# A hybrid attention layer in one kernel: one product of ones per gated norm, transposes taken in pairs, and head 0's mixes, its v and the end's logarithm in other places

## The chip, the cores and the metric

The kernel runs on one core of a Trainium2 chip. The metric is the time of one execution on the device in microseconds (us). The engines are named as in the profile: PE is TensorE (matrix products and transposes), PEld its weight loads, DVE is VectorE, ACT is ScalarE, POOL is GpSimd, SP is SyncE, which here only issues DMA transfers. Each engine works off its own queue of instructions in order and waits for others through semaphores.

## The reference

One layer of a decoder trunk: 1024 positions, width 1024, eight heads of differential softmax attention beside four heads of gated linear attention (GLA), all in float32. Cut to what matters:

```python
h = rms_norm(x, pre_g)
z = h @ w_in                        # qa ka va ga | qb kb vb gb gk_low
# differential attention, 8 heads, two maps of 64 each, v of 128
p = softmax(where(mask, s, -inf))   # for both maps, causal
w = p[:, :, 0] - lam * p[:, :, 1]
oa = rms_norm(w @ v, subln_g) * (1 - lam_init) * silu(ga)
# gated linear attention, 4 heads, keys of 128, values of 256
ob = gla_chunked(qb, kb, vb, log_sigmoid(gk) / 16)
ob = rms_norm(ob, gla_g) * silu(gb)
y = concatenate([oa, ob]) @ w_out
return x + rms_norm(y, post_g)
```

## The kernel before

Float32 accuracy is reached by splitting: an operand is cast to a rounded form (`_hi`) and the rest (`_lo`) is what the cast left; products of hi and lo parts are summed in a PSUM bank. So each operand costs a cast on ACT and a subtraction on DVE.

The work has four stages by the trace: the loads and the first norm (to 16 us), the projections with GLA between them (to 616 us), the attention (616 to about 912 us), and the last products and the final norm (to 963 us). Everything is written as generators that yield costs; a merger interleaves them, and a scheduler then sets the order on each engine, except for instructions marked `keep_in_program_order`, which stay in order among themselves. `issue_after(x)` puts an instruction behind x.

In GLA, each of eight units (four heads, two halves of the positions) ends in a norm: the squares of its 256 values lie as two tiles of 128 rows, which are added to `sq`, split into `sq_hl` (hi and lo, 128 rows each), and summed over the rows by two products with a matrix of ones, into a bank called `gms`. In the attention the same norm (`attn_norm`, bank `ms`) already folds its 128 rows to 64, and puts hi and lo one below the other, so that one product does.

The attention's streams:

- `scores(h, qb)`: for head h and query block qb (7 down to 0), the scores of both maps m into one of three banks `sc`, then on DVE a masked reduce to `p0` or `p1` (the custom instruction, printed ISA in the order of instructions), which also leaves a bound in `stt`; on ACT the Exp, which leaves the sum of a row in `stt`; on DVE the RECIPROCAL of both maps' sums; on POOL p1 times lambda; on DVE the mix of both maps (SCALAR_TENSOR_TENSOR `p<-p,stt,p`). In head 0 the mixes of the blocks above 3 are held in a list and made behind a later block's reduce.
- `all_values()`: for each head, half 1 of the queries and then half 0, in units of one block of keys (the last unit has two): `turn` transposes the mixed maps into one of two banks `wtr` (TR) and takes them out as `wt_hi` (cast on ACT) and `wt_lo` (DVE); `weigh` multiplies with v into the one bank `po`. Transposes run two units ahead. At the end of a half `po` is copied to `o`, which frees the bank, and the norm follows; its result, `gate`, is stored to `mixd`. The norm's bank `ms` is taken in turn from the same two as the transposes.
- early products of the output projection (`ypart`, `yps`), which fill TensorE's time between the scores. From about 793 us on they also use the attention's own results, which are loaded from `mixd` as `m_raw` and split into `m_hi` and `m_lo` in `mix_part`.

Loads by SP wait for each other only through their data and through the buffers that they fill. `turned_last` and `squared_last` name the instructions behind which some of the end's ACT work is held.

Of the kernel before, what the change touches and what calls it, by code (L numbers as in the profile page):

```python
# [14 lines left out]
P = 128  # L15
# [16 lines left out]
def hymba_kernel(  # L32
# [44 lines left out]
    def fp(t):  # L77
        return t.bitcast(F32)
# [930 lines left out]
    def gla(g):  # L1009

        u = None
        for half in range(2):
# [72 lines left out]
            dve.tensor_tensor(sq, sqs[:, 0], sqs[:, 1], ALU.add)  # L1085
            hl = kp.tile([P, 2, 512], F32R, tag="k1", name="sq_hl")
            act.copy(hl[:, 0], sq)
            dve.tensor_tensor(hl[:, 1], sq, fp(hl[:, 0]), ALU.subtract)
            for _ in range(2 if last else 3):
                yield  # L1090
            ms, ib = take_bank([P, 512], "gms")
            for i in range(2):
                mm(ms, ones, hl[:, i], start=(i == 0), stop=(i == 1))
            r = t_c("r")
# [143 lines left out]
    def load_v(h):  # L1238
        v = [smp.tile([P, NT, P], F32R, tag="v", name=f"v{t}", bufs=4) for t in range(2)]
        for t in range(2):  # L1240

            with tc.issue_after(qk_load[0]) if h else nullcontext():
                ins = sp.dma_start(fp(v[t]), v_d[h // 4][h % 4, t])
            if h == 0:
                tc.keep_in_program_order(ins)
        return v

    v_first = load_v(0)

# [13 lines left out]
    def scores(h, qb):  # L1263
# [6 lines left out]
        for m, p in enumerate((p0, p1)):  # L1270
# [5 lines left out]
            for i, (a, b) in enumerate(parts):  # L1276
# [21 lines left out]
                if (h, qb) == (0, NT - 1):  # L1298
                    lowest[:] = [ins.ins]
                c = 0.08 + (e - a) / 512 * 0.56  # L1300
                if last:
                    act.activation(
                        p[:, :n], p[:, :n], AF.Exp, bias=st[:, m : m + 1], scale=-1.0,
                        accum_out=st[:, 2 + m : 3 + m],
                    )
                if last and m:
                    dve.reciprocal(st[:, 4:6], st[:, 2:4])
                    pool.tensor_scalar(
                        p1[:, :n], p1[:, :n], st[:, 5:6], lam, ALU.mult, ALU.mult
                    )  # L1310
                    while mixed:
                        with tc.issue_after(ins.ins):
                            mixed.pop()()

                    def mix_maps():
                        dve.scalar_tensor_tensor(
                            p0[:, :n], p0[:, :n], st[:, 4:5], p1[:, :n], ALU.mult, ALU.subtract
                        )
                        w[h, qb] = p0

                    if h == 0 and qb > 3:
                        mixed.append(mix_maps)
# [5 lines left out]
    lowest, mixed = [], []  # L1328

    def all_scores():  # L1330
        for h in range(DA_HEADS):
            for qb in range(NT - 1, -1, -1):
# [3 lines left out]
                if qb == 4 and h + 1 < DA_HEADS:  # L1336
                    for n in ("q", "k", "ks"):
                        load_qk(h + 1, n, 1)
                    for n in ("k", "ks"):
                        load_qk(h + 1, n, 0)  # L1340
# [9 lines left out]
    def turn(h, half, kts):  # L1350
# [3 lines left out]
        for kt in kts:  # L1354
            for i in blocks_of(kt, half):
                tr(pt[:, n : n + P], w[h, 4 * half + i][:, kt * P : (kt + 1) * P])
                n += P
        hi = smp.tile([P, 512], F32R, tag="wt_hi", name="wt_hi", bufs=3)
        lo = smp.tile([P, 512], F32R, tag="wt_lo", name="wt_lo", bufs=3)
# [19 lines left out]

    def attn_norm(h, half, o):  # L1380
        if h < DA_HEADS - 1:
# [14 lines left out]
        dve.tensor_tensor(sq[:64], sq[:64], fold[:64], ALU.add)  # L1396
        ins = act.copy(hl[:64], sq[:64]).ins
        if ending:
            squared_last.append(ins)
        dve.tensor_tensor(hl[64:], sq[:64], fp(hl[:64]), ALU.subtract)  # L1400
# [11 lines left out]
        act.activation(r, ms, AF.Ln, bias=eps_t, scale=1.0 / P)  # L1412
        act.activation(r, r, AF.Exp, scale=-0.5)
        if h < DA_HEADS - 1:
# [9 lines left out]
    def all_values():  # L1424


        AHEAD = 2
# [4 lines left out]
        vs, os, turned, norms_todo = {0: v_first}, {}, {}, []  # L1432
        ahead = iter(units)
# [8 lines left out]
        for i, (h, half, kts) in enumerate(units):  # L1442
            last = kts[-1] == 4 * half + 3

            ahead_by = AHEAD if h < DA_HEADS - 1 else AHEAD
# [12 lines left out]
            weigh(po, half, kts, vs[h], turned[h, half, kts])  # L1458
            norm_step()
            if last:  # L1460
                act.copy(o, po)
                if half and h + 1 < DA_HEADS:
                    vs[h + 1] = load_v(h + 1)
                norms_todo.append(attn_norm(h, half, o))
            yield 0.6
# [330 lines left out]
```

## Time and profile before

| | us |
|---|---|
| median of 3 runs | 965.65 (965.34 to 966.77) |
| the profiled execution | 964.64 |
| its span | 962.9 |
| PE busy | 953.0 (99%) |
| DVE busy | 736.6 (76%) |
| ACT busy | 603.6 (63%) |
| POOL busy | 199.0 (21%) |

The span goes from the first instruction to the last in the profile; the 1.7 us between it and the execution's own time lie around it. The mean granted clock of TensorE is 0.998 of full speed. A row of a timeline gives the start, the duration, the engine, the line, the operation with the tile it writes and those it reads, the shape, and in brackets the idle time of the engine just before and what ended it. The line is often that of a helper (L66, L142, L145), so groups are told apart by their tiles.

### The profile page before, as it was taken

The page shows a single profiled execution, that of the slowest core. Times are in us where ns is not written, and L with a number is a line of the kernel's source. Part 1 is how long each engine was busy: PE and PEld are TensorE (multiplying, and loading weights), DVE is VectorE, ACT ScalarE, POOL GpSimd, SP SyncE. Part 2 cuts the span into 40 slices and gives each one's busy share as a digit, 9 for nine tenths or more (in the row PEclk, how much of TensorE's full clock was granted, in tenths as well). Part 3 has the DMA queues.
Part 4 walks back from the last instruction along what each step waited for, and adds up shares of the span by engine and source line. Part 5 has one row for each costly group of instructions (what it writes and reads, how often), then busy time and mean ns, then how long its engine had stood idle before and what let it go on. Part 6 is the DMA issues. An engine that isn't in the chain of part 4 may idle for free.

```text
span 962.9 us, 14404 instructions
## 1 busy us (share of the span) xinstructions
PE 953.0 (99%) x4640; PEld 795.9 (83%) x4640; DVE 736.6 (76%) x1468; ACT 603.6 (63%) x1166; POOL 199.0 (21%) x264
## 2 busy tenths in 40 slices
PE   9999999999999999999999999999999999999997
PEld 7887788888888888888888888878888888888875
DVE  5898799996678687687667576587888888898554
ACT  8753355845677556577765344366777787787773
POOL 3101002122142112111100002122222222433321
PEclk9999999999999999999999999999999999999999
DMA  9616367487577897985754498996666669994767
GB/s 343 217 35 167 91 196 253 163 299 246 189 251 239 281 309 236 299 285 193 259 175 145 151 291 273 408 305 198 219 207 208 220 226 357 320 292 104 162 196 149
DMA packets 152827, 220.36 MB, mean 229 GB/s; under 512 B 15728, under 2 KB 85360, under 8 KB 152656
## 3 DMA queue, kind: packets, MB, share of 16 engines
q1 hardware_dynamic: 138304, 177.65, 57.5%
q0 software_dynamic: 14448, 41.79, 14.9%
q8 instruction: 37, 0.61, 0.3%
q14 instruction: 38, 0.31, 0.1%
HBM read 133.93 MB, written 88.60 MB: 231 GB/s over the span
## 4 chain that ended last, share of the span: by engine, by line
PE 96%; ACT 1%; DVE 1%; DMA 1%; issue 0%; SPq 0%; DVEq 0%; ACTq 0%
PE x L142 24%; PE y L142 16%; PE z L142 16%; PE ypart L142 13%; PE sc L142 7%; PE po L142 5%; PE yps L142 4%; PE wtr L145 3%; PE gpo L142 3%; PE kv L142 1%; PE gkl_ps L142 1%; PE pa L142 1%; DMA x<-in_x_dram 1%; PE xT L145 1%; DVE p L66 1%
## 5 line engine op out<-in xcount | busy, mean ns | idle before, releaser
L66 ACT CAST w<-w_raw 128x512 fp32r<-128x512 f32 x138 | 85.2, 621 | 76.8 <-PE y L142 33.6
L66 DVE TENSOR_TENSOR w<-w_raw,w 128x512 fp32r<-128x512 f32 x138 | 94.1, 685 | 38.4 <-ACT w L66 38.2
L66 ACT ACTIVATE p<-p,stt 128x896 f32<-128x896 f32 (+7 forms) x128 | 99.3, 776 | 34.3 <-DVE stt L66 33.0
L66 ACT COPY s<-x 128x512 f32<-128x512 f32 x78 | 44.8, 587 | 74.2 <-PE x L142 74.0
L66 DVE CUSTOM_DVE_ANT_0 p<-sc,maskt 128x512 f32<-128x512 f32 (+3 forms) x128 | 74.3, 585 | 16.0 <-PE sc L142 14.6
L66 POOL TENSOR_SCALAR p<-p,stt,lam 128x1024 f32<-128x1024 f32 (+3 forms) x64 | 56.4, 882 | 144.8 <-DVE stt L66 144.1
L142 PE MATMUL z<-s_hi,w 128*128 128x512 f32 x320 | 80.2, 393 | 0.0
L142 PE MATMUL x<-s_hi,w 128*128 128x512 f32 x320 | 80.1, 392 | 0.0
L142 PE MATMUL y<-h_hi,w 128*128 128x512 f32 x320 | 80.1, 392 | 0.0
L142 PE MATMUL ypart<-wo_hi,m_hi 128*128 128x512 f32 x192 | 79.5, 414 | 0.1
L142 PE MATMUL ypart<-wo_hi,m_lo 128*128 128x512 f32 x192 | 75.5, 393 | 0.0
L142 PE MATMUL ypart<-wo_lo,m_hi 128*128 128x512 f32 x192 | 75.4, 393 | 0.0
L66 POOL DMA_DIRECT2D wo_d<-wo_hi x32 | 17.4, 544 | 275.0 <-ACT wo_hi L66 275.0
L142 PEld LDWEIGHTS z<-s_hi,w 128*128 128x128 f32 x320 | 59.8, 188 | 12.4
L142 PEld LDWEIGHTS x<-s_hi,w 128*128 128x128 f32 x320 | 59.7, 188 | 12.4
L142 PEld LDWEIGHTS y<-h_hi,w 128*128 128x128 f32 x320 | 59.7, 188 | 12.3
L142 PE MATMUL sc<-k,q 128*128 128x512 f32 (+1 forms) x192 | 68.7, 362 | 0.6 <-DVE stt L66 0.6
L142 PE MATMUL sc<-ks,q 128*128 128x512 f32 (+1 forms) x192 | 66.1, 347 | 0.0
L66 ACT CAST wt_hi<-wtr 128x512 fp32r<-128x512 f32 (+1 forms) x80 | 42.8, 535 | 27.1 <-PE wtr L145 26.1
L66 DVE TENSOR_TENSOR wt_lo<-wtr,wt_hi 128x512 fp32r<-128x512 f32 (+1 forms) x80 | 50.6, 632 | 9.0 <-ACT wt_hi L66 8.5
L66 DVE TENSOR_TENSOR w_raw<-w_raw 128x512 f32<-128x512 f32 x80 | 55.2, 690 | 1.2 <-DMA w_raw<-in_w_in_dram 0.2
L66 DVE TENSOR_TENSOR c<-z,s 128x512 f32<-128x512 f32 x48 | 32.8, 687 | 29.8 <-ACT s L66 19.9
(232 smaller groups left out, 2352.0 us busy)
## 6 DMA issues: line engine op xcount, KB each, us to landing
w_raw<-in_w_in_dram SPq DMA_DIRECT2D x40, 512.0 KB, 5.0
wo_d<-wo_hi POOLq DMA_DIRECT2D x32, 256.0 KB, 3.3
q<-q_d SPq DMA_DIRECT2D x32, 256.0 KB, 4.8
k<-k_d SPq DMA_DIRECT2D x32, 256.0 KB, 5.4
ks<-k_d SPq DMA_DIRECT2D x64, 128.0 KB, 5.9
v<-v_d SPq DMA_DIRECT2D x16, 512.0 KB, 6.5
wo_raw<-in_w_out_dram POOLq DMA_DIRECT2D x31, 256.0 KB, 4.8
wo_d<-gqd POOLq DMA_DIRECT2D x22, 256.0 KB, 4.2
```

Of the source, the lines that this page charges most:

```text
L66: ins = op(*a, **k)
L142: tc.keep_in_program_order(pe.matmul(*a, **k))
L145: tc.keep_in_program_order(pe.transpose(dst, src, ident))
```

## The change

- Gated norms: the squares' upper 64 rows are copied down and added to the lower 64, hi and lo lie in one tile of 128 rows, and one product of ones replaces two.
- `all_values()`: the transposes of two units stand in a row, into both TR banks. The second unit's take-out, where it runs furthest ahead, comes behind the values product of the present unit.
- Head 0: all reduces are kept in program order; the mix of block qb is made behind a given reduce of a lower block (7 behind (5, 0), 6 behind (4, 0), 5 behind (4, 1), 4 behind (3, 1), 3 behind (1, 0), 2 behind (0, 0)) instead of from a list. v of head 0 is loaded behind head 1's second-half queries instead of first.
- The end: the last copy of `o` waits until the half-1 norm's Exp has been issued, instead of the norm's Ln and Exp coming behind the copy.

```diff
@@ the gated norm @@
-            hl = kp.tile([P, 2, 512], F32R, tag="k1", name="sq_hl")
-            act.copy(hl[:, 0], sq)
-            dve.tensor_tensor(hl[:, 1], sq, fp(hl[:, 0]), ALU.subtract)
+            act.copy(sqs[:64, 1], sq[64:])
+            dve.tensor_tensor(sq[:64], sq[:64], sqs[:64, 1], ALU.add)
+            hl = kp.tile([P, 2, 512], F32R, tag="k1", name="sq_hl")[:, 0]
+            act.copy(hl[:64], sq[:64])
+            dve.tensor_tensor(hl[64:], sq[:64], fp(hl[:64]), ALU.subtract)
...
-            for i in range(2):
-                mm(ms, ones, hl[:, i], start=(i == 0), stop=(i == 1))
+            mm(ms, ones, hl, start=True, stop=True)
@@ load_v, scores @@
-    v_first = load_v(0)
...
+                if h == 0:
+                    tc.keep_in_program_order(ins)
                 c = 0.08 + (e - a) / 512 * 0.56
+                if last and (qb, m) in mixed:
+                    with tc.issue_after(ins.ins):
+                        mixed.pop((qb, m))()
...
-                    while mixed:
-                        with tc.issue_after(ins.ins):
-                            mixed.pop()()
...
-                    if h == 0 and qb > 3:
-                        mixed.append(mix_maps)
+                    if h == 0 and qb > 1:
+                        mixed[(qb - 1, 1) if qb in (4, 5) else (qb - 2, 0)] = mix_maps
...
-                    for n in ("q", "k", "ks"):
+                    load_qk(h + 1, "q", 1)
+                    if not h:
+                        vs[0] = load_v(0)
+                    for n in ("k", "ks"):
                         load_qk(h + 1, n, 1)
@@ attn_norm @@
+        if h == DA_HEADS - 1 and not half:
+            with tc.issue_after(squared_last[0]):
+                act.copy(o, po)
...
-        ins = act.copy(hl[:64], sq[:64]).ins
-        if ending:
-            squared_last.append(ins)
+        act.copy(hl[:64], sq[:64])
...
-        act.activation(r, r, AF.Exp, scale=-0.5)
+        ins = act.activation(r, r, AF.Exp, scale=-0.5).ins
+        if ending:
+            squared_last.append(ins)
@@ all_values @@
-            while len(turned) < min(i + 1 + ahead_by, len(units)):
-                u = next(ahead)
-                if u[2] == (0,):
-                    yield lambda: (u[0], 4 * u[1]) in w
-                turned[u] = turn(*u)
-                if u[2][-1] == 4 * u[1] + 3:
-                    used.add(u[:2])
-                yield 0.4
-                norm_step()
+            late = None
+            while len(turned) < min(i + 3, len(units)):
+                pair = [next(ahead), next(ahead)]
+                for u in pair:
+                    if u[2] == (0,):
+                        yield lambda: (u[0], 4 * u[1]) in w
+                pts = [turn(*u) for u in pair]
+                for u, pt in zip(pair, pts):
+                    if len(turned) == i + 3:
+                        late, turned[u] = (u, pt), None
+                    else:
+                        turned[u] = take_out(*pt)
+                    if u[2][-1] == 4 * u[1] + 3:
+                        used.add(u[:2])
+                yield 0.8
+                norm_step()
+                norm_step()
...
             weigh(po, half, kts, vs[h], turned[h, half, kts])
+            if late:
+                turned[late[0]] = take_out(*late[1])
```

`turn` now ends with the transposes, and `take_out` is what was its second part: the cast to `wt_hi` and the subtraction for `wt_lo`.

The change also moves instructions that the diff does not name, since the scheduler orders them anew. Three places follow; numbers behind the names tell tiles apart and differ between the two programs.

VectorE in head 0, before: block 7 (`stt_5861`), its last reduce and the first of block 6 (`stt_5896`). The rows of shape 128x1 read an accumulator.

```order
L66 ISA p1_5863,stt_5861<-sc_5883,maskt_78,stt_5861 128x512
L66 ISA stt_5861 128x1
L66 ISA p0_5897,stt_5896<-sc_5899,maskt_78 128x512
L66 ISA stt_5896 128x1
L66 ISA p0_5897,stt_5896<-sc_5903,maskt_78,stt_5896 128x384
L66 ISA stt_5896 128x1
L66 RECIPROCAL stt_5861<-stt_5861 128x2
L66 ISA p1_5898,stt_5896<-sc_5908,maskt_78 128x512
```

The same place after, with block 7 as `stt_5865` and block 6 as `stt_5900`:

```order
L66 ISA p1_5867,stt_5865<-sc_5887,maskt_78,stt_5865 128x512
L66 ISA stt_5865 128x1
L66 RECIPROCAL stt_5865<-stt_5865 128x2
L66 ISA p0_5901,stt_5900<-sc_5903,maskt_78 128x512
L66 ISA stt_5900 128x1
L66 ISA p0_5901,stt_5900<-sc_5907,maskt_78,stt_5900 128x384
L66 ISA stt_5900 128x1
L66 ISA p1_5902,stt_5900<-sc_5912,maskt_78 128x512
```

Block 7's RECIPROCAL moved from behind two reduces of block 6 to directly behind its own block's last reduce; the same holds for blocks 6, 5, 4 and 3, with their mixes further behind.

ScalarE around 790 to 798 us, before: the Exp of block 6 of a head (`p0_7932`, `p1_7933`, 896 wide), the norm (`r`), take-outs, and the first cast of `m_raw`.

```order
L66 CAST wt_hi_7943<-wtr_7938 128x512
L66 ACTIVATE r_7965<-ms_7963,eps_t_76 128x512
L66 ACTIVATE r_7965<-r_7965 128x512
L66 ACTIVATE p0_7932,stt_7931<-p0_7932,stt_7931 128x896
L66 CAST wt_hi_7989<-wtr_7985 128x384
L66 ACTIVATE p1_7933,stt_7931<-p1_7933,stt_7931 128x896
L66 CAST m_hi_8186<-m_raw_7916 128x512
```

After, with the same work as `p0_7940`, `p1_7941`, `r_7988`, `wt_hi_7955` and `wt_hi_7997`:

```order
L66 CAST wt_hi_7955<-wtr_7946 128x512
L66 CAST m_hi_8194<-m_raw_7924 128x512
L66 ACTIVATE p0_7940,stt_7939<-p0_7940,stt_7939 128x896
L66 ACTIVATE r_7988<-ms_7986,eps_t_76 128x512
L66 CAST wt_hi_7997<-wtr_7951 128x384
L66 ACTIVATE r_7988<-r_7988 128x512
L66 ACTIVATE p1_7941,stt_7939<-p1_7941,stt_7939 128x896
```

The cast of `m_raw` moved ahead of five instructions. On TensorE, the transposes behind (shape 128x384, three of them) keep their place in the queue, row 2499 in both programs; they now write the bank that `wt_hi_7997` empties.

TensorE in the last head, before, where half 1 of the queries ends (`po_9237`) and half 0 begins (`po_9419`):

```order
L142 MATMUL po_9237<-wt_hi_9323,v0_9054 128x128
L142 MATMUL po_9237<-wt_hi_9323,v1_9055 128x128
L142 MATMUL po_9237<-wt_lo_9324,v0_9054 128x128
L142 MATMUL ypart_9348<-wo_hi_8051,m_hi_9209 128x512
L142 MATMUL ypart_9348<-wo_hi_8051,m_lo_9210 128x512
L142 MATMUL ypart_9348<-wo_lo_8052,m_hi_9209 128x512
L145 MATMUL wtr_9379<-ident_71,p0_9107 128x128
L145 MATMUL wtr_9379<-ident_71,p0_9070 128x128 x2
L142 MATMUL po_9419<-wt_hi_9341,v0_9054 128x512
L142 MATMUL po_9419<-wt_hi_9341,v1_9055 128x512
L142 MATMUL po_9419<-wt_lo_9342,v0_9054 128x512
```

After, the same as `po_9253` and `po_9416`:

```order
L142 MATMUL po_9253<-wt_hi_9336,v0_9078 128x128
L142 MATMUL po_9253<-wt_hi_9336,v1_9079 128x128
L142 MATMUL po_9253<-wt_lo_9337,v0_9078 128x128
L142 MATMUL po_9416<-wt_hi_9346,v0_9078 128x512
L142 MATMUL po_9416<-wt_hi_9346,v1_9079 128x512
L142 MATMUL po_9416<-wt_lo_9347,v0_9078 128x512
```

The products and the transposes that stood between the last product of one half and the first of the next are gone from between them; the copy of `po` to `o` is needed between the two in both programs. In the other heads, where two to four microseconds of TensorE's work stood at this place, 1.15 us (four heads) and 1.84 us (three heads) of products and transposes remain.

More of the change, by code (lines that the diff above doesn't have):

```diff
@@ L1240, in load_v @@
         for t in range(2):
[L1242 to L1245, printed above, removed]
+            with tc.issue_after(qk_load[0]):
+                sp.dma_start(fp(v[t]), v_d[h // 4][h % 4, t])
         return v
-    v_first = load_v(0)
     n_sc, n_tr = [0], [0]
@@ L1326, in scores @@
                 yield c
-    lowest, mixed = [], []
+    lowest, mixed, vs = [], {}, {}
     def all_scores():
@@ L1357, in turn, with take_out @@
                 n += P
+        return pt, n
+    def take_out(pt, n):
         hi = smp.tile([P, 512], F32R, tag="wt_hi", name="wt_hi", bufs=3)
@@ L1378, in weigh, with attn_norm @@
             n += ns
-    def attn_norm(h, half, o):
+    def attn_norm(h, half, o, po):
+        if h == DA_HEADS - 1 and not half:
+            with tc.issue_after(squared_last[0]):
+                act.copy(o, po)
         if h < DA_HEADS - 1:
@@ L1424, in all_values @@
     def all_values():
-        AHEAD = 2
         units = [
@@ L1431, in all_values @@
         ]
-        vs, os, turned, norms_todo = {0: v_first}, {}, {}, []
+        os, turned, norms_todo = {}, {}, []
         ahead = iter(units)
@@ L1443, in all_values @@
             last = kts[-1] == 4 * half + 3
-            ahead_by = AHEAD if h < DA_HEADS - 1 else AHEAD
-            while len(turned) < min(i + 1 + ahead_by, len(units)):
-                u = next(ahead)
-                if u[2] == (0,):
-                    yield lambda: (u[0], 4 * u[1]) in w
-                turned[u] = turn(*u)
-                if u[2][-1] == 4 * u[1] + 3:
-                    used.add(u[:2])
-                yield 0.4
+            late = None
[14 more added lines that the diff above has]
+                norm_step()
                 norm_step()
@@ L1458, in all_values @@
             weigh(po, half, kts, vs[h], turned[h, half, kts])
+            if late:
+                turned[late[0]] = take_out(*late[1])
             norm_step()
             if last:
-                act.copy(o, po)
+                if i + 1 < len(units):
+                    act.copy(o, po)
                 if half and h + 1 < DA_HEADS:
                     vs[h + 1] = load_v(h + 1)
-                norms_todo.append(attn_norm(h, half, o))
+                norms_todo.append(attn_norm(h, half, o, po))
             yield 0.6
```

## The prediction

> **What bounds the kernel now.** I read the head of the page first, for the busy shares and the granted clock; then the chain that ended last; then TensorE's waits by releaser; then the timelines of the three places that the change reorders.
>
> ```profile
> span 962.9 us, 14404 instructions
> ...
> PE 953.0 (99%) x4640; PEld 795.9 (83%) x4640; DVE 736.6 (76%) x1468; ACT 603.6 (63%) x1166; POOL 199.0 (21%) x264
> ...
> PEclk9999999999999999999999999999999999999999
> ...
> PE 96%; ACT 1%; DVE 1%; DMA 1%; issue 0%; SPq 0%; DVEq 0%; ACTq 0%
> ```
>
> TensorE (PE) is busy for 99% of the span, its clock is at the top digit in all forty slices, and 96% of the chain is its own work. So the time is the sum of what TensorE issues plus the few places where it stands still. A change gains only what it takes out of TensorE's queue or out of those stalls, and it loses whatever new stall it makes. The stalls that exist are short:
>
> ```profile
> PE spin L142 <- POOL idle L66: 1.5, 1, 1.5
> PE sc L142 <- DVE stt L66: 0.6, 2, 0.4
> PE wtr L145 <- DVE p L66: 0.4, 1, 0.4
> PE yps L142 <- ACT m_hi L66: 0.3, 1, 0.3
> PE xT L145 <- DVE x L66: 0.2, 1, 0.2
> PE yps L142 <- DVE m_lo L66: 0.2, 1, 0.2
> ```
>
> The columns are total microseconds, times, longest. Beside the start there is 0.6 + 0.4 us in head 0 (score banks and the first mixed map) and 0.3 + 0.2 us at the end: 1.5 us is all that better ordering can win back. With so little idle, the other engines are close behind TensorE, and an instruction put one or two places too early in the VectorE (DVE) or ScalarE (ACT) queue has almost no slack to spend.
>
> **The gated norms' product.** Eight norms each send one product of ones fewer.
>
> ```profile
> 150.59 2.72 PE x L142 x12
> 407.42 0.68 DVE L66 TENSOR_TENSOR sq_hl<-sq,sq_hl 128x512 fp32r<-128x512 f32 x1
> 410.55 0.64 PE L142 MATMUL gms<-sq_hl,ones 128*128 128x512 f32 x2
> ```
>
> In the chain, twelve 128x512 products take 2.72 us, so 0.227 us each; 8 × 0.227 = 1.8 us leave TensorE's queue. The norm gains one ScalarE copy and one VectorE add, about 0.6 to 0.7 us each by the row of the same form at 407.42. Here that row ends at 408.10 and the product starts at 410.55, 2.45 us later, so 1.3 us more still fits. It is hidden by the projection's products standing between; without them it would be 8 × 1.3 us. Term: -1.8 us, ends -1.8 and 0.
>
> **Transposes in pairs.** [...] I take -0.2 us, ends -0.4 and 0. In exchange both transpose banks fill at once, and the norm's product (ms) of every head's half now takes the next bank, which must first be emptied by a copy and a subtraction. Before shows no such wait; the nearest stall is the 0.4 us one on a mixed map above, and 16 norms × 0.4 = 6.4 us is the far end, 0 the near one. At most places some 2 us of TensorE's work stands between the pair and the norm, more than one copy, so I take +0.8 us.
>
> **The accumulator (po) between two halves.** Pairing also moves the accumulator's last product of one half close to the first of the next.
>
> ```profile
> 907.41 0.27 PE L142 MATMUL po<-wt_lo,v 128*128 128x128 f32 x1
> ...
> 907.72 0.59 ACT L66 COPY o<-po 128x512 f32<-128x512 f32 x1 [0.85 <-PE po L142]
> ```
>
> The copy that empties the bank starts 0.3 us after the last product's start and takes 0.6: the next half can begin 0.9 us after that start at the earliest. In the order of before, three products and a transpose group stand between in the last head, two to four microseconds elsewhere. Now nothing stands between in the last head: 0.9 less the product's own 0.1, with a signal's delay, +1.0 us (ends 0.8, and 1.9 if one Exp is ahead of the copy). In the other seven heads one and a half to two units remain, 1.15 us of products at four and 1.84 at three. With one 0.6 us instruction ahead of the copy, the four wait 0.9 + 0.6 - 1.15 = 0.35 us each, 1.4 in all; with none, 0. I take +1.0, ends 0 and 4.2 (an Exp of 1.15 us ahead everywhere).
>
> **Head 0.** All of head 0's score reduces are now kept in program order, and each RECIPROCAL now stands directly behind the last reduce of its own block.
>
> ```profile
> 623.50 0.69 DVE L66 CUSTOM_DVE_ANT_0 p<-sc,maskt 128x512 f32<-128x512 f32 x1 [0.44 <-PE sc L142]
> ...
> 624.89 0.16 DVE L66 RECIPROCAL stt<-stt 128x2 f32<-128x2 f32 x1
> ...
> 627.77 0.68 DVE L66 CUSTOM_DVE_ANT_0 p<-sc,maskt 128x512 f32<-128x512 f32 x1
> ...
> 631.05 0.69 DVE L66 CUSTOM_DVE_ANT_0 p<-sc,maskt 128x512 f32<-128x512 f32 x1
> ...
> 633.55 1.02 DVE L66 SCALAR_TENSOR_TENSOR p<-p,stt,p 128x768 f32<-128x768 f32 x1 [0.59 <-POOL p L66]
> ...
> 789.99 0.17 DVE L66 RECIPROCAL stt<-stt 128x2 f32<-128x2 f32 x1 [1.08 <-ACT p L66]
> ```
>
> ```profile
> 623.10 1.15 ACT L66 ACTIVATE p<-p,stt 128x1024 f32<-128x1024 f32 x1 [0.27 <-DVE stt L66]
> ...
> 626.69 1.05 ACT L66 ACTIVATE p<-p,stt 128x896 f32<-128x896 f32 x1 [0.54 <-DVE stt L66]
> ...
> 630.64 0.92 ACT L66 ACTIVATE p<-p,stt 128x768 f32<-128x768 f32 x1
> ```
>
> ```profile
> 631.80 0.33 PE L142 MATMUL sc<-k,q 128*128 128x128 f32 x1 [0.24 <-DVE stt L66]
> ...
> 637.72 0.66 PE L145 MATMUL wtr<-ident,p 128*128 128x128 f32 x4 [0.40 <-DVE p L66]
> ```
>
> A RECIPROCAL needs the sums of both maps, which the Exp of the second map leaves. The row at 789.99 shows what happens where it stands close behind: VectorE idled 1.08 us for ScalarE. In head 0 before, the reduces of the next block stood in between (623.50 to 624.89) and covered the Exp of 623.10. Now they stand behind it. Walk in the clock of before: the Exp begun at 623.10 takes 1.15 and about 0.1 more for reading its sum, so block 6's first reduce goes from 623.50 to 624.5. Its second map also takes a buffer that now lies over other staging tiles, those of the last query stores:
>
> ```profile
> 613.32 8.65 SPq L482 DMA_DIRECT2D q_d<-qk_st  x8
> ...
> DMA to landing us min/median/max: 5.2/7.8/9.3
> ```
>
> The last of the eight is issued near 621.5 and lands at least 5.2 us later, 626.7: the reduce that could run at 625.75 (two reduces of 0.6 on) waits about 1.0 us. After block 6's Exp and RECIPROCAL (about 629.5), block 5 starts at 629.55 instead of 627.77; with its mixed map and Exp, block 4's first reduce starts near 634.5 instead of 631.05, 3.4 us late. TensorE has three score banks and stood waiting for exactly these reduces already (631.80), so it is late by as much. The first transposes (637.72) move by 2.5 to 3.4 us, and a mix now ahead of block 0's reduce adds a wait for POOL like the 0.59 one. Set up as a ledger it agrees: new idles of about 1.4, 1.25, 1.1, 0.15 and 0.9 us, less those of 0.4, 0.4, 0.6, 0.45 and 0.2 that they replace, are 2.8; with 1.2 at the mixes +4.0. Ends: -1.0 (the 0.6 + 0.4 us of stalls go and the waits stay under the three banks' lead) and +4.9 (all new idles, nothing replaced).
>
> The loads of v(0) move behind head 1's queries in SP's queue, past head 1's second-half keys. The same bytes pass, v is wanted at the first values product after the first transposes, itself later now. I take 0, hidden by those 2.5 us; without that cover one landing of about 5 us less its lead, up to 2 us, is in the range only.
>
> **The casts of m_raw.** Here the diff says nothing, but the order of ScalarE does: the first cast m_hi<-m_raw of the end's products now stands ahead of two Exp, the norm's Ln and Exp and a take-out, five instructions earlier.
>
> ```profile
> 787.25 0.56 SPq L1417 DMA_DIRECT2D mixd<-gate  x1
> ...
> 793.55 1.47 SPq L1489 DMA_DIRECT2D m_raw<-mixd  x3
> ```
>
> ```profile
> DMA to landing us min/median/max: 3.3/5.2/9.2
> ```
>
> ```profile
> 791.64 0.59 ACT L66 CAST wt_hi<-wtr 128x512 fp32r<-128x512 f32 x1 [0.70 <-PE wtr L145]
> 793.38 0.69 ACT L66 ACTIVATE r<-ms,eps_t 128x512 f32<-128x512 f32 x1 [1.15 <-PE ms L142]
> ...
> 795.16 1.04 ACT L66 ACTIVATE p<-p,stt 128x896 f32<-128x896 f32 x1 [0.42 <-DVE stt L66]
> ...
> 796.20 0.46 ACT L66 CAST wt_hi<-wtr 128x384 fp32r<-128x384 f32 x1
> ...
> 798.08 0.60 ACT L66 CAST m_hi<-m_raw 128x512 fp32r<-128x512 f32 x1
> ```
>
> ```profile
> 796.85 0.56 DVE L66 TENSOR_TENSOR wt_lo<-wtr,wt_hi 128x384 fp32r<-128x384 f32 x1
> ```
>
> ```profile
> 797.34 0.49 PE L145 MATMUL wtr<-ident,p 128*128 128x128 f32 x3
> ```
>
> The store to mixd is issued at 787.25, the read of it waits for its landing and is issued at 793.55; 798.08 is 4.5 us on, under the median landing of 5.2 (the middle line), so the data can hardly be there earlier. ScalarE would be ready for the cast after the take-out of 791.64, at 792.2: it stands still for 5.8 us. Then come the cast (0.5), Exp (1.05), Ln (0.69), take-out (0.46), and VectorE's subtraction (0.56): 798.08 + 3.2 = 801.3. The transposes of TensorE at 797.34 stand at the same place of its queue after as before, and now need the bank which that take-out empties. Term: 801.3 - 797.3 = +4.0 us; ends 0 (data there before ScalarE asks) and 5.8 (no lead at all).
>
> [...]
>
> ```profile
> 1.53 5.97 PE L142 MATMUL spin<-idle,ones 128*128 128x512 f32 x14 [1.53 <-POOL idle L66]
> ```
>
> At the start fourteen products take 5.97 us, 0.427 each against 0.227 later, so TensorE can run at half speed; no stall of before after the start exceeds 0.4 us, and no row shows whether 4 us would bring that back. [...]
>
> **The end.** The half-1 norm's logarithm and gate go ahead of the last copy of o and of the casts. That removes the 0.3 us wait for m_hi and the 0.2 us for m_lo of the rows above, and puts the last copy and the next casts later by about 1.3 us of Ln and Exp; one of the final products then waits for its seed. Term: -0.2 us, ends -0.5 and +1.0.
>
> **The sum.** -1.8 - 0.2 + 0.8 + 1.0 + 1.0 + 4.0 + 4.0 - 0.2 = +8.6 us on the profiled execution of 964.64 us (span 962.9 and 1.7 around it): 973.2. The median of the runs is 965.65, 1.0 above that execution, so 974.3 us.
>
> **The rivals.** (1) The casts are covered: m_raw lands before ScalarE asks, because the store or the read is issued sooner or SP's queue is freer there. For: the landing's least is 3.3 us. Against: both transfers would have to gain nearly 6 us together. Then 4.0 goes: 970.3 us.
> (2) The stall at the cast also puts TensorE back to the rate of the start for as long as there: 14 × (0.427 - 0.227) = 2.8 us, 977.1 us. For: the start's row. Against: the clock line never falls in this trace. [...]
> (3) Faster: pinned reduces free the three score banks in the order in which TensorE asks for them. Before, block 5's second map was reduced ahead of the first's end, and TensorE waited at 631.80 for a bank freed out of turn. If that was the limit in head 0, its 0.6 + 0.4 us vanish with 1.8 us of products: 965.65 - 2.8 = 962.8 us. It decides if VectorE's wait at each RECIPROCAL stays under the three banks' lead, 6 products × 0.227 = 1.4 us. Against: the leads were already used up at 631.80 and the waits add up over five blocks. It needs the casts covered as well.
> (4) No difference: head 0 loses half of my sum, the casts nothing, small terms cancel: -1.8 + 2.0 = 965.8 us.
>
> **How the numbers follow.** My sum 0.48; rival (1) 0.24; (2) 0.11; (3) 0.08; (4) 0.09. About 0.2% (1.9 us) can be told from no change, so slower holds the first three, 0.83, same 0.09, faster 0.08. My own case spans 971 to 979 by the ends of its two large terms (head 0 down by 1, casts down by 2; banks and accumulator up by 4). The range reaches down to 966.5 to take in rival (1) and the upper part of (4), and up to 982, with rival (2) and the accumulator's far end; outside lie (3), half of (4) and a few hundredths above.
>
> **What the changed profile would show.** Eight gms products. In head 0, RECIPROCAL rows with 0.7 to 1.3 us of idle released by ACT's p, and one reduce released by a store of qk_st; TensorE's waits on stt grown from 0.6 us to about 4. Near 800, an m_hi row with 5 us or more of idle released by m_raw's DMA and a wait of some 4 us on a transpose; a lower clock digit or longer products behind it would speak for (2). At the last accumulators a wait on ACT's o of about 1 us. I am wrong if RECIPROCAL idles do not reach TensorE, if m_hi's idle is under 2 us, or if a wait stands in a place that I costed at nothing, such as v(0) or the norm's bank.

## The result and the profile after

The changed kernel takes 979.39 us (median of 5 runs, 976.11 to 981.02) against 965.65 (965.27 to 966.77): ratio 1.0135, 95% interval 1.0116 to 1.0154, 13.7 us slower. The execution with the profile is the one of 979.39 us, 14.75 more than that of before. The forecast was 974.3 us, range 966.5 to 982.0. Direction and range held; the size was 5 us short.

The head of the page and TensorE's waits, for the rows shown of before:

```profile
span 977.7 us, 14428 instructions
...
PE 956.3 (98%) x4632; PEld 796.2 (81%) x4632; DVE 746.2 (76%) x1476; ACT 608.5 (62%) x1174; POOL 199.1 (20%) x264
...
PEclk9999999999999999999999999999999999999999
```

```profile
PE sc L142 <- DVE stt L66: 4.0, 5, 1.3
PE ms L142 <- DVE wt_lo L66: 3.3, 2, 2.9
PE wtr L145 <- DVE wt_lo L66: 2.1, 1, 2.1
...
PE po L142 <- ACT o L66: 0.9, 1, 0.9
...
PE yps L142 <- ACT yps L66: 0.5, 1, 0.5
PE ms L142 <- DVE sq_hl L66: 0.5, 1, 0.5
```

Eight products fewer (4632 for 4640), and yet TensorE's busy time grew from 953.0 to 956.3 us. Each forecast stall is there: the score banks (4.0 us for 0.6; 3.3 of it in head 0 and 0.7 at 697 us), the transposes behind the early cast (2.1), the last half's accumulator (0.9). The norm's product (ms), to which the forecast gave 0.8 us in all, has the longest single wait, 2.9 us.

A part of this growth comes from how busy time is counted: a product's duration, 0.39 us with a modelled end, counts in full ahead of a stall, and as the 0.23 us to the next start where products follow each other. The other part is not in the clock line, whose digits stand for 24 us each, but in narrow stretches (columns: stretch, its length, busy time and instructions of PE, PEld, DVE, ACT and POOL, granted clock, DMA share and GB/s):

```profile
622.00:629.00 7.00, 5.35 (x23) 3.46 (x22) 3.65 (x13) 2.40 (x6) 2.00 (x2) 1.00 0.83 233
629.00:632.40 3.40, 3.40 (x10) 2.73 (x10) 2.70 (x7) 1.34 (x3) 0.27 (x1) 0.50 0.77 246
...
840.60:844.00 3.40, 3.36 (x8) 2.72 (x9) 2.33 (x6) 2.87 (x6) 0.00 (x0) 0.51 1.09 315
844.00:850.00 6.00, 6.00 (x33) 5.04 (x33) 3.22 (x9) 1.38 (x4) 3.18 (x3) 0.99 0.89 262
```

Twice, for 3.4 us each, the granted clock is half. In the first stretch TensorE is busy throughout with 10 products. I come back to this after the experiments.

A ledger of the profiled execution by TensorE's rows: for each product the time to the next one's start, less the usual time for its kind, summed over stretches, after less before.

| stretch, us | what stands there | more than before, us |
|---|---|---|
| 400 to 520 | two folded norms, waits of 0.2 | +0.5 |
| 615 to 660 | head 0, with 1.6 of half clock | +5.8 |
| 680 to 720 | a score bank (0.8), accumulator | +1.3 |
| 760 to 800 | norm's product (0.3), early product's bank (0.6) | +0.9 |
| 800 to 820 | transposes behind the cast | +2.6 |
| 820 to 860 | norm's product (3.1 of wait, 0.3 of its own), half clock (1.4) | +5.1 |
| 860 to 900 | a norm's product (0.5) | +0.4 |
| 900 to 977 | a norm's product 0.6, accumulator 1.1, a seed 0.8, less before's 1.2 at the casts | +1.5 |
| | the start (-0.7) and the rest | -1.1 |
| | eight products and the transposes fewer | -2.2 |

The rows sum to +14.8, the executions differ by 14.75.

### The profile page after: what moved, and what is told of

It is laid out like the page before. It is cut to its first block, busy times and chain, and to the rows that moved or that the text cites. A ratio compares the mean times of both kernels' runs of the same rounds, so it can differ in the third digit from the quotient of the medians.

```text
span 977.7 us, 14428 instructions
## 1 busy us (share of the span) xinstructions
PE 956.3 (98%) x4632; PEld 796.2 (81%) x4632; DVE 746.2 (76%) x1476; ACT 608.5 (62%) x1174; POOL 199.1 (20%) x264
## 4 chain that ended last, share of the span: by engine, by line
PE 87%; DVE 5%; ACT 3%; DMA 3%; issue 1%; SPq 0%; POOL 0%; DVEq 0%; ACTq 0%
PE x L142 23%; PE y L142 15%; PE z L142 15%; PE ypart L142 10%; PE sc L142 5%; PE po L142 5%; PE yps L142 4%; PE gpo L142 3%; PE wtr L145 2%; DVE p L66 2%; PE kv L142 1%; ACT p L66 1%; DMA k_d<-qk_st 1%; PE gkl_ps L142 1%; PE pa L142 1%
```

## The experiments

What was expected stands as it was written before each run. "Alone" means the kernel before with that part only. Each time stands beside runs of the kernel before on the same chip: 964.67 in the first four, 964.93 in the next four, 965.51 for the two after these and for the last one, 964.98 for the one with RECIPROCAL later.

**The folded norms alone.** The first two hunks of the diff.

> The kernel before with the folded gated norms alone. Theory A (the parts add up; each stall has its own cause): eight products of 0.227 us go, 1.8 us, and the changed profile shows two gms products waiting 0.2 to 0.25 us with a slower pair behind, 0.5 us together, so 1.3 us less than before, about 964.4 us. Rival B (the folded norm's two further steps are covered everywhere): 1.8 us less, 963.8 us. Rival C (the projections are bounded by VectorE, and its eight further adds of 0.68 us reach the end): no gain or up to 3 us more.

962.96 us (11 runs), ratio 0.998 (0.9971 to 0.9988): 1.7 us less, between A and B; C falls. The profile has waits of 0.2 us at two of the eight norms (409 and 517 us).

**Head 0's part alone.** The hunks of `load_v`, `scores` and of the loads.

> The kernel before with head 0's part alone (reduces in program order, mixes in their new places, v of head 0 loaded later). Theory A: the stalls between 615 and 650 us come with it and nothing else does: 5.8 us more than before, of which some 1.5 are products at 0.427 us instead of 0.227; about 971.5 us, and no stall above 0.6 us near 800 and 840. Rival B (head 0's delay also puts the later loads and casts out of step): a part of the stalls at 800 and 840 appears too, 974 us or more. Rival C (the stalls of head 0 need the pairs of transposes): under 2 us more.

970.31 us (967.95 to 970.78), ratio 1.0046 (1.0033 to 1.0059), 5.6 more: A. Its longest stalls beyond 650 us are before's two at the end. In VectorE's timeline, the RECIPROCALs of blocks 7, 6 and 5 wait for the Exp, and one reduce for a landing:

```profile
624.49 0.17 DVE L66 RECIPROCAL stt<-stt 128x2 f32<-128x2 f32 x1 [1.36 <-ACT p L66]
...
626.45 0.69 DVE L66 CUSTOM_DVE_ANT_0 p<-sc,maskt 128x512 f32<-128x512 f32 x1 [0.42 <-DMA q_d<-qk_st]
...
629.16 0.17 DVE L66 RECIPROCAL stt<-stt 128x2 f32<-128x2 f32 x1 [1.25 <-ACT p L66]
...
634.39 0.17 DVE L66 RECIPROCAL stt<-stt 128x2 f32<-128x2 f32 x1 [1.16 <-ACT p L66]
```

Its five runs fall into two groups: 967.95 and 968.14 at a mean granted clock of 0.999, and 970.31 to 970.78 at 0.997 to 0.998. The profile is of the first group and has no slow products behind these stalls, so its 3.5 us are stalls alone.

**The pairs alone.** The hunks of `turn`, `take_out` and of the loop in `all_values`.

> The kernel before with the transposes in pairs alone. ScalarE's order then has the first cast of m_raw five instructions early, as in the changed kernel. Theory A: the stalls at 697, 800, 837 and at the last half's accumulator come with it: about 1.3 + 0.9 + 2.6 + 5.1 + 0.5 + 1.1 = 11.5 us more than before by the changed profile's stretches, or some 1.4 less where the products behind the stall near 840 stay at full rate: 974 to 977 us. Head 0 shows before's stalls. Rival B (pairs need head 0's delay to come out of step): under 4 us more.

976.14 us (975.40 to 978.55), ratio 1.0119 (1.0105 to 1.0133): 11.5 more, A. The stalls of the changed kernel from 690 us on are all there without head 0's delay, but for the seed's, which belongs to the end's part; the two longest have almost the same length (4.25 us of idle ahead of the cast on ScalarE, 2.95 us ahead of ms on TensorE). Head 0 has two waits for take-outs near 641 us (0.4 and 0.7 us) that A didn't have.

```profile
799.11 0.62 ACT L66 CAST m_hi<-m_raw 128x512 fp32r<-128x512 f32 x1 [4.25 <-DMA m_raw<-mixd]
```

```profile
839.57 0.47 PE L142 MATMUL ms<-sq_hl,ones 128*128 128x512 f32 x1 [2.95 <-DVE wt_lo L66]
```

In this profile the clock is half behind the cast's stall as well, which it is not in the changed kernel (same columns as above):

```profile
799.84:803.25 3.41, 1.17 (x10) 0.90 (x9) 2.43 (x5) 3.41 (x8) 0.15 (x1) 1.00 0.94 299
803.25:806.66 3.41, 3.41 (x11) 2.73 (x11) 1.89 (x6) 1.40 (x4) 2.21 (x2) 0.50 1.01 360
```

**The end's part alone.** `attn_norm`'s copy of `o` behind the norm's Exp.

> The kernel before with the end's part alone (norm's logarithm and Exp ahead of the last copy of o). Theory A: the 0.5 and 0.6 us stalls at the casts of 918 us go, and one stall of about 0.7 us on a copy of yps comes: 0.3 to 0.5 us less, 965.2 us. Rival B: without the pairs the last copy of o comes late for the end's seeds, up to 1 us more.

964.49 us (11 runs), ratio 0.9998 (0.9989 to 1.0007): no difference that can be told. The waits of yps on m_hi and m_lo (0.5 us together) went and one on a copy of yps came (0.5 us), as A has it.

The four parts add up to -1.7 + 5.6 + 11.5 - 0.2 = 15.2 us against 13.7 together. So nearly all of the loss is in two parts, each by itself, and they don't need each other.

**Head 0 without the fixed order of reduces.** Head 0's part less these two lines:

```diff
-                if h == 0:
-                    tc.keep_in_program_order(ins)
```

> Head 0's part alone without keeping the reduces in program order: the mixes stand in their new places and v of head 0 is loaded late, but in VectorE's order each RECIPROCAL of blocks 7 to 4 stands one or two reduces behind its block again. Theory A (TensorE's stalls in head 0 come from VectorE waiting at RECIPROCAL for the Exp of its own block): no RECIPROCAL idle above 0.5 us but one wait for a query store's landing stays; 964.5 to 966 us. Rival B (the new places of the mixes or the later load of v cost the time): 969 to 971 us, as the whole part.

968.41 us (966.88 to 969.76), ratio 1.0029 (1.0018 to 1.0040), 3.5 more. A missed. The RECIPROCALs of blocks 7 and 6 wait 0 and 0.64 us, but the wait for the stores' landing is longer (1.63 us). With the 0.64 us it makes TensorE wait 2.2 us for score banks, and 3.4 us at half clock follow (635.27 to 638.68 us):

```profile
625.15 0.16 DVE L66 RECIPROCAL stt<-stt 128x2 f32<-128x2 f32 x1
626.94 0.69 DVE L66 CUSTOM_DVE_ANT_0 p<-sc,maskt 128x512 f32<-128x512 f32 x1 [1.63 <-DMA q_d<-qk_st]
...
629.66 0.17 DVE L66 RECIPROCAL stt<-stt 128x2 f32<-128x2 f32 x1 [0.64 <-ACT p L66]
```

**Head 0 with v loaded first.** Head 0's part with `v_first = load_v(0)` and the loads' order of before.

> Head 0's part alone, with v of head 0 loaded first as before, so that the p1 buffers don't lie over the query stores' staging; reduces in program order, each RECIPROCAL directly behind its block. Theory A: the RECIPROCAL idles of about 1.2 us stay, the wait for the stores' landing (1.5 us in the changed profile) goes: about 1.0 to 1.5 us less than the whole part's 970.3, 969 us. Rival B (the wait for the landing starts the row of delays and the RECIPROCALs are hidden without it): 965 to 966 us.

968.14 us (967.28 to 968.90), ratio 1.0027 (1.0016 to 1.0038), 3.2 more. No wait for a landing, RECIPROCAL idles of 1.31, 1.20 and 1.16 us and a later one of 1.67, TensorE's waits for score banks 2.9 us. Nearer to A (969) than to B: the RECIPROCALs cost without the landing too. Here too 3.4 us at half clock follow (634.40 to 637.81 us). So head 0 has two causes; each alone brought 2.2 us of stalls or more and, in its profiled execution, 3.4 us at half clock behind them, over 3 us together, and they overlap: 3.5 + 3.2 are 6.7, both at once 5.6. VectorE is late by the one or by the other, and the second finds part of its wait already passed: the landing's wait is 0.42 us behind a RECIPROCAL idle of 1.36 and 1.63 us behind none.

**The pairs with the cast held back.** In `mix_part`, with `last_r` the Exp of the latest norm:

```diff
-        pin(pool_d, act.copy(hi[:, :n, :], raw[:, :n, :]))
+        with tc.issue_after(last_r[0]) if not pool_d else nullcontext():
+            pin(pool_d, act.copy(hi[:, :n, :], raw[:, :n, :]))
```

> The pairs alone, with each cast of m_raw held behind the last norm's Exp: on ScalarE the first cast moves behind one Exp, the norm's Ln and Exp and a take-out; TensorE's order is the same. Theory A (ScalarE stands for m_raw's landing and with it the take-out for which the transposes wait): the 2.4 us stall near 800 goes to under 0.5, and where the clock had dropped behind it, that goes too: 973 to 974 us against 976.1 with the pairs alone. Rival B (the transposes wait because both banks are full, whatever the cast does): 975.5 to 976.5 us.

973.37 us (972.62 to 974.36), ratio 1.0080 (1.0067 to 1.0093), 2.8 less than the pairs alone; the two intervals don't overlap. A: TensorE has no stall of over 0.2 us between 794 and 832, and the half clock of 803.25 to 806.66 us is gone too. Not all of the 2.8 us is the cast: the long wait of ms is 2.1 us here for 2.95. The cast now stands behind the norm's Exp and waits for nothing:

```profile
798.37 0.69 ACT L66 ACTIVATE r<-ms,eps_t 128x512 f32<-128x512 f32 x1
798.96 0.47 ACT L66 CAST wt_hi<-wtr 128x384 fp32r<-128x384 f32 x1
799.32 0.64 ACT L66 ACTIVATE r<-r 128x512 f32<-128x512 f32 x1
799.85 0.62 ACT L66 CAST m_hi<-m_raw 128x512 fp32r<-128x512 f32 x1
```

**Pairs, but not while a norm is pending.**

```diff
-                pair = [next(ahead), next(ahead)]
+                pair = [next(ahead)] if norms_todo else [u for u in (next(ahead), next(ahead, None)) if u]
...
-                yield 0.8
-                norm_step()
-                norm_step()
+                yield 0.4 * len(pair)
+                for _ in pair:
+                    norm_step()
```

> The pairs alone, but while a norm is pending units are transposed one by one as before, so that the norm's product finds an empty bank; ScalarE's order has the first cast of m_raw at before's place again. Theory A (the norm's product meets two full banks): the waits of ms on wt_lo and sq_hl (3.1 + 0.5 + 0.6 + 0.3 us in the pairs' profile) go, with them the slow products behind 840 us, and the 2.4 us at 800; what stays is the accumulator's 1.1 and two stalls of 0.8 to 0.9 us near 642 and 695: 966.5 to 968 us. Rival B (VectorE and ScalarE are simply too full for pairs): 972 us or more.

966.09 us (11 runs), ratio 1.0007 (0.9999 to 1.0016): 10 of the 11.5 us are gone, a little more than A had. Of the 40 pairs 19 are still there (the 80 units stand in 61 groups of transposes), and they cost little. No wait of ms is left; the accumulator's wait and the one near 695 us, which A left, are gone too. ScalarE's order has the cast at before's place again, so its early place was a consequence of the pairs at the norm, not a separate edit.

**Folded norms and end.** Both parts, nothing else.

> The folded norms and the end's part together, without the pairs and without head 0's part. Theory A (the parts add up): -1.7 us by the folded norms alone and -0.2 by the end alone, 1.9 us less than the kernel before, about 962.9 us. Rival B (the end's part only shifts a wait, no gain beside the fold): 963.1 to 963.5 us.

962.78 us, ratio 0.9973 (0.9962 to 0.9983): the fastest version here, 2.7 us under the kernel before of its runs. Beside the folded norms alone (962.96, on another chip) the end's part can't be told from nothing.

**The same with the mixes' new places.** With `mixed` as a table, v first and no fixed order.

> As the version with the folded norms and the end's part, and with head 0's mixes at their new places, but with v loaded first and the reduces not kept in order, so that neither the wait for the stores' landing nor the RECIPROCAL directly behind its block comes with it. Theory A (the mixes' places are neutral or gain some of head 0's 2 us of stalls): 962 to 963 us. Rival B (the new places of the mixes cost time by themselves): 964 us or more.

963.21 us (962.44 to 964.18), ratio 0.9977 (0.9967 to 0.9986): the places of the mixes are neutral, A's first half, though the time is 0.2 us above A's range.

**RECIPROCAL later.** The version with folded norms, end, mixes and fixed order; RECIPROCAL and POOL's product of blocks 7 to 4 are put in a table like the mixes:

```diff
+                if h == 0 and last and (qb, m) in recips:
+                    with tc.issue_after(ins.ins):
+                        recips.pop((qb, m))()
...
+                    if h == 0 and qb > 3:
+                        recips[qb - 1, 0] = turn_sums
+                    else:
+                        turn_sums()
```

> The folded norms and the end's part, and head 0's reduces in program order with the mixes at their new places and v loaded first; but the RECIPROCAL of blocks 7 to 4, with POOL's product behind it, is made behind the first map's last reduce of the next block. Against the version with v first this moves four RECIPROCALs and nothing else in VectorE's order of reduces. Theory A (the idle at the RECIPROCALs is head 0's cost, and reduces in TensorE's order cost nothing by themselves): VectorE's idles of 1.2 us for ScalarE go, TensorE's stalls on score banks fall from 2.9 us to under 1; 962 to 963.2 us, at or under the 962.8 of folded norms and end. Rival B (reduces in program order or the mixes' places cost by themselves): 964.5 us or more.

964.22 us (11 runs), ratio 0.9994 (0.9985 to 1.0003). The idles at these RECIPROCALs are gone, but TensorE still waits 1.3 us for score banks where before has 0.6:

```profile
622.89 0.16 DVE L66 RECIPROCAL stt<-stt 128x2 f32<-128x2 f32 x1
...
626.10 0.48 DVE L66 CUSTOM_DVE_ANT_0 p<-sc,maskt,stt 128x256 f32<-128x256 f32 x1 [0.83 <-PE sc L142]
...
626.51 0.16 DVE L66 RECIPROCAL stt<-stt 128x2 f32<-128x2 f32 x1
```

Neither theory has it: the time lies between theirs. Beside the version with the mixes' new places, which differs by the fixed order and by where RECIPROCAL stands, it loses 1.6 us by ratios (0.9994 for 0.9977) and 1.0 by medians; the two intervals just touch, so even this rest is not certain. Where RECIPROCAL stood directly behind its block, 3.2 us were lost beside the kernel before. Reduces in TensorE's order gain nothing by themselves; what the rest of the loss is, I can't say from these runs (one row shows VectorE now waiting 0.83 us for scores that TensorE makes later).

**Eight stalls.** The folded norms alone, with a chain of POOL instructions ahead of each product of ones:

```diff
+            for _ in range((7, 5, 7, 5, 4, 8, 6, 5)[2 * g + half]):
+                pool.tensor_scalar(hl, fp(hl), 1.0, 1.0, ALU.mult, ALU.mult)
```

> The folded norms alone, and in each of the eight gated norms a chain of four to eight POOL multiplications by one on the folded tile ahead of the product of ones, so that TensorE stands still once in each norm, for some 1.5 to 3.6 us by POOL's 0.83 us for such an instruction, between products of full length. It asks from which stall on the products behind run at 0.427 us instead of 0.227. [...] Time about 20 to 28 us more than the folded norms alone.

1000.39 us, ratio 1.0361 (1.0342 to 1.0380), 35 us more than the kernel before. The stalls came out longer than planned, 1.98 to 4.4 us by TensorE's waits, so what shorter ones do stays open. The two shortest, in TensorE's timeline:

```profile
392.72 0.50 PE L142 MATMUL gms<-sq_hl,ones 128*128 128x512 f32 x1 [2.37 <-POOL sq_hl L66]
393.06 1.11 PE L142 MATMUL x<-s_hi,w 128*128 128x512 f32 x4
```

```profile
513.01 0.51 PE L142 MATMUL gms<-sq_hl,ones 128*128 128x512 f32 x1 [1.98 <-POOL sq_hl L66]
513.36 3.28 PE L142 MATMUL x<-s_hi,w 128*128 128x512 f32 x8
```

Behind the longer of the two, four products take 1.11 us; behind the shorter, eight take 3.28, and the granted clock of the stretch is half:

```profile
393.00:396.40 3.40, 3.40 (x16) 2.75 (x16) 2.65 (x5) 1.68 (x3) 0.00 (x0) 1.00 0.02 8
...
513.70:517.00 3.30, 3.30 (x10) 2.54 (x9) 2.06 (x4) 1.19 (x3) 0.00 (x0) 0.51 0.21 79
```

Seven of the eight stalls were followed by slow products (the execution's mean granted clock is 0.984, before's 0.998 to 0.999). Length alone doesn't decide: the one that was not, of 2.37 us, is longer than the one of 1.98.

## Why the prediction was right in direction and short in size

- **What bounds the kernel: right.** Every microsecond lost is a stall of TensorE or a product at half rate.
- **Folded norms, -1.8: right.** Alone they bring -1.7.
- **Transposes in pairs, -0.2:** no row of before's shows a saving, and the profiles after show none at most places: four transposes in a row take 0.44 us before, eight 0.88 after. Only the eight rows of six are shorter than two of three, 0.60 us for 0.66. That is too small to tell; what the pairs set off is not.
- **The banks behind the pairs, +0.8: this step failed.** The sum held "some 2 us of TensorE's work" against "one copy" and so took almost no wait for the norm's product. The wait is not for one copy but for the queues in which the take-out stands. Near 837 us the transposes of the pair go at 833.90, the take-out's subtraction ends at 840.5, behind these on VectorE:

```profile
836.23 1.09 DVE L66 TENSOR_TENSOR m_lo<-m_raw,m_hi 128x512 fp32r<-128x512 f32 x1 [0.23 <-ACT m_hi L66]
837.24 1.27 DVE L66 SCALAR_TENSOR_TENSOR p<-p,stt,p 128x1024 f32<-128x1024 f32 x1
838.55 0.69 DVE L66 TENSOR_TENSOR sq_hl<-sq,sq_hl 64x512 fp32r<-64x512 f32 x1
839.26 0.62 DVE L66 CUSTOM_DVE_ANT_0 p<-sc,maskt,stt 128x384 f32<-128x384 f32 x1
...
839.81 0.69 DVE L66 TENSOR_TENSOR wt_lo<-wtr,wt_hi 128x512 fp32r<-128x512 f32 x1
```

```profile
840.64 0.75 PE L142 MATMUL ms<-sq_hl,ones 128*128 128x512 f32 x1 [2.94 <-DVE wt_lo L66]
```

  The four such norms measured 0.3, 3.1, 0.5 and 0.6 us, 4.5 in all, and 1.4 of half clock behind the long one. I had the far end (6.4) and took 0.8, close to the near one, without walking a single place through VectorE's queue, as I had done for the casts. A wait on the norm's bank was among the prediction's own signs of being wrong, and it came. The version without pairs at norms shows what it was worth, with the cast, the last accumulator and the stall near 695 us: 10 us.
- **The accumulator, +1.0 and +1.0: right.** The last head's product waited 0.95 us on the copy of `o`:

```profile
923.69 0.73 PE L142 MATMUL po<-wt_hi,v 128*128 128x512 f32 x2 [0.95 <-ACT o L66]
```

  It starts 0.05 us behind the copy's end (923.64), which is what this profile shows of the signal's delay in the sum. The seven others came to some 0.7 by the reckoning of the ledger; the profile lists no wait there.
- **Head 0, +4.0: right in cause, and 4.2 without the clock.** The profile of the changed kernel has RECIPROCAL idles of 1.25 and 1.16 us and a reduce 1.50 us behind the stores' landing, and TensorE's waits on stt in head 0 grew from 0.6 to 3.3. The working counted the landing as a delay of 1.0 inside the row of RECIPROCALs; the runs show two causes that stand in for each other, so it is in part luck that the size came out this close.
- **The casts, +4.0: right in mechanism, too large.** The chain behind the data is as worked out, and TensorE waits on its last link:

```profile
801.75 0.62 ACT L66 CAST m_hi<-m_raw 128x512 fp32r<-128x512 f32 x1 [4.14 <-DMA m_raw<-mixd]
...
803.88 0.46 ACT L66 CAST wt_hi<-wtr 128x384 fp32r<-128x384 f32 x1
```

```profile
804.99 0.98 PE L145 MATMUL wtr<-ident,p 128*128 128x128 f32 x7 [2.14 <-DVE wt_lo L66]
```

  From the data at 801.75 to the transposes it is 3.24 us, 3.2 in the sum. But TensorE asked 0.9 us behind the data here and not 0.75 ahead of it as by before's rows: the chain started from two points of one clock that had shifted against each other. Holding back the cast in the pairs alone brought 2.8 us, with the half clock that stood behind it in their profile.
- **The end, -0.2:** alone it has the forecast waits, and its time can't be told from no change; in the whole the seed's stall (0.8 us) stands for before's 1.2.
- **Loads of v, 0: wrong in its reason.** The move of v cost by the buffers that it shifted, not by v's own landing: with v first the wait for the stores' landing is gone and head 0's part costs 3.2 us for 5.6. That cost was counted under head 0.
- **A stall that I hadn't listed:** 0.8 us on a score bank at 697, which the pairs bring alone too.
- **Rival (2), the clock: it came true.** In the changed kernel it came behind head 0 and behind the norm's product, 1.6 + 1.4 us, and not behind the cast's stall to which I had tied it; with the pairs alone it came there too. What I held against it, that the clock line never falls, could not decide: 3.4 us at half clock lower a digit's 24 us by 7%, and the digit stays 9. With those 3.0 us my sum of 8.6 would have been 11.6 of the 14.75. The rest is the banks (3.7 more than I took) and the stall at 697 (0.8), less the casts (1.4) and small terms of both signs. That the time lies in the range although the banks were short and the clock was left out is partly owed to the casts, which were too large.
- **Rival (1)** falls with ScalarE's 4.14 us of idle ahead of the cast, **rival (4)** with the whole's time. **Rival (3):** reduces in TensorE's order do not free the banks sooner even where VectorE hardly waits at a RECIPROCAL (0.22 us once in head 0, in the version with RECIPROCAL later).

## What to carry to other kernels

Where TensorE is full, read what a change does to the order of the engines behind it: an instruction moved a few places forward in a queue that works in order waits there for its own input, and holds up everything behind it (4.14 us at the early cast here). Two buffers filled in a row leave none for the third user that took turns with them, and its wait can be as long as the whole queue in which the emptying stands (2.94 us at the norm's product); walk that queue at one place before giving it a number. Try each part of a change alone: here one part gained 1.7 us, and two lost 5.6 and 11.5.

## What the runs showed of the hardware

TensorE's rate fell to half behind waits that are shorter than the 4 us of which the prediction asked: in the changed kernel behind two of 0.27 and 1.28 us in head 0 and behind the 2.94 us at the norm's product. Products of 512 columns then start 0.427 us apart instead of 0.227. Each time this lasts 3.41 us there, 629.03 to 632.45 and 840.66 to 844.07 us, and as long in the pairs alone (803.25 to 806.66), in head 0 without the fixed order (635.27 to 638.68) and with v first (634.40 to 637.81). The traces also record when the granted clock changes. In the changed kernel's it is full from 4.39 to 629.03, from 632.45 to 840.66 and from 844.07 to 973.78 us: 624.64, 208.21 and 129.71 us, which are 183, 61 and 38 times 3.413. In before's it is full for 952.32 us in one piece, 279 times 3.413. What sets these lengths, the traces don't show.

The length of a wait alone doesn't say whether slow products follow. Of the eight stalls the one of 1.98 us (513.01) was followed by them and the one of 2.37 us (392.72) was not. In the changed kernel the 2.14 us at the cast (804.99) were followed by none: from 806.51 us on the products start 0.23 us apart. As an estimate from the starts in TensorE's rows, with 0.227 us for a product of 512 columns and their share of it for others, TensorE stood still for 2.46 of the 3.41 us ahead of the slow stretch in head 0 (the two waits and smaller gaps), for 3.12 of the 3.41 us ahead of the one at 840.66, and for 2.32 of the 3.41 us from 803.11 to 806.52 us, behind which the clock stayed full. From how much standstill on the rate falls was not shown.

In two kernels the times of the runs go with the clock, though only one run of each version has a trace: head 0 alone took 967.95 and 968.14 us at a mean granted clock of 0.999, and 970.31 to 970.78 at 0.997 to 0.998; the changed kernel took 976.11 and 977.66 us at 0.998, and 979.39 to 981.02 at 0.995. Its runs spread over 4.9 us where those of before spread over 1.5.
